# A one-core layer kernel: GpSimd's computing steps behind the routing go to VectorE and ScalarE, and one load moves

## The chip, the cores and the metric

The kernel runs on one core of a Trainium2 chip. The metric is the device time of one execution in microseconds (us). The core has TensorE (PE in the profile; PEld is its weight load), VectorE (DVE), ScalarE (ACT), GpSimd (POOL) and SyncE (SP), which here only issues DMAs. Each engine works through its own instructions in program order and waits for the others by semaphores.

## The reference

One transformer layer for 512 tokens of width 2048, float32. Three mixers run on one input projection, their outputs go through a projection, are added to the input and normed. A router then gives each token two of 32 experts, and the experts' weighted outputs are added and normed again:

```python
x = layer_norm(ALPHA * x + mix, ln1_g, ln1_b)
probs = softmax(x @ wg_r + bg_r)              # 4 groups, the best one is taken
e_val, e_idx = top_k(expert logits in that group, 2)
gates = g_val * softmax(e_val)
for each expert e, on the tokens routed to it:
    h = silu(xb @ w_gate[e]) * (xb @ w_up[e])
    ffn[token] += gate * (h @ w_down[e])
out = layer_norm(ALPHA * x + ffn, ln2_g, ln2_b)
```

## The kernel before, in words

The 512 tokens are four blocks (`b`) of 128 partitions; a block's row is 2048 wide, and `H` are its two halves, `Q` its four quarters. Matmuls are float32 in three parts: each operand is split by ScalarE into a rounded high part and by VectorE into the rest (lines 96 and 97 for weights, in the class `Ring`; 161 and 162 in `split`), and `mm3` (156 to 158) sums three products. Weights come in chunks of 512 KB. `Ring` holds a list of raw buffers and of split pairs: `pump` issues a chunk's load on the sync queue when a raw buffer is free (line 81) and splits it when a pair is free; `done` gives a used pair back and pumps. The order of all work is the order of the code, per engine.

**Routing** (lines 1099 to 1281). For each block `stats` (line 1106 on) makes the first norm's statistics (BATCH_NORM_STATS2, line 1006), `ln1` (1086) the normed rows, which go to the DRAM tensors `x1d` (one for each half); `route` makes one-hot choices in many small VectorE steps (lines 1129 to 1160), and `ranks`, `table` turn them into a table `idx` of the token for each expert and slot, with counts `cnt_i`. The last block's chain runs behind the last matmul of the projection. `xgs` are two buffers of 128 rows (in the slots M0 and B3) into which an expert's tokens are gathered; GpSimd clears both at line 1203. `exps` (1254 to 1257) has two exponentials of ScalarE behind two small GpSimd steps.

**Experts.** `gather(e)` (1322) issues two indirect DMAs on GpSimd's queue, for as many rows as the expert has tokens, rounded up to one of eight sizes; rows past that keep what the buffer held, and their gate is zero. From the third expert on GpSimd clears the buffer first (1330). `rows` transposes the rows on TensorE (1350) and applies the first norm's gain (1366, 1439). `up(e)` (1372) runs the gate and up matmuls for all 16 chunks; an expert with at most 64 tokens takes two matmuls for a piece of weights (1392, 1393), others three (`mm3`). `down(e)` (1414) runs the down projection, scales it by the gate table `gt` (1432), and `scatter` adds the rows to the DRAM tensors `yd` by indirect DMAs with an add (1340). `up(e)` is followed by `down(e - 1)`; at the end come `down(30)` and `down(31)`. The hooks of `up` put other steps between its chunks. `gates` is one of them, spread over chunks 0, 5 and 7 of the first expert's second half: a product over 128x256 (1284), a high part by ScalarE (1287), the rest of it by GpSimd (1288), eight matmuls (1292) that make the table of gates `gt`.

**Vectors.** `gb1` are two buffers (slots X7, B2) that hold the first norm's gain and bias from expert 12 on; VectorE applies them to the residual rows `z` during experts 13 to 28 (1562). At expert 29 the second norm's two vectors are loaded into the same slots (1557), on the sync queue, broadcast to all partitions, 1 MB each.

**The end** (from line 1577). The sums of the experts are read back from `yd` into `ys` (1581): seven reads on the sync queue, one on GpSimd's; a read of a half waits for the last scatter into that half. Then the second norm: `add` (1632) adds the sums to `z` and sums the row, `mean` (1589), `squares` (ScalarE, 1641), `root` (1594, 1595), `refine` (1600 to 1608) sharpens the root, `norm` (1613) and `scale_dve` (1620) apply it on VectorE in halves and store. A part goes to the other engines: block 3's adds to GpSimd (`add_pool`, 1635) with ScalarE's `total` (1638), block 1's norm and the last quarter of block 3 to ScalarE (`norm_act`, 1625) and GpSimd (`gain`, 1629).

Of the kernel before, what the change touches and what calls it, by code (L numbers as in the profile page):

```python
# [9 lines left out]
F32 = mybir.dt.float32  # L10
# [3 lines left out]
AF = mybir.ActivationFunctionType  # L14
OP = mybir.AluOpType
# [5 lines left out]
P = 128  # L21
T = 512
NB = T // P
DM = 2048
KD = DM // P
NE = 32
# [11 lines left out]
EPS2 = EPS / ALPHA ** 2  # L38
# [96 lines left out]
def _build(tc, nc, ctx, I, out):  # L135
# [8 lines left out]
    def slot(tag, shape, dt=F32):  # L144
        cnt[0] += 1
        return bp.tile([P] + list(shape), dt, tag=tag, name=f"{tag}_{cnt[0]}")
# [6 lines left out]
    act = nc.scalar.activation  # L153
# [73 lines left out]
    for k2 in range(8):  # L227
        t = slot(f"X{k2}", [2, 2, 512], F32R)
# [48 lines left out]
    def bcast(ap, n):  # L277
        return bass.AP(tensor=ap.tensor, offset=ap.offset, ap=[[0, P], [1, n]])
# [566 lines left out]
    def scale(b, Pn, s):  # L845
        nc.vector.reciprocal(s, s)
        ts(Pn[b], Pn[b], s, None, op0=OP.mult)
# [234 lines left out]
    def wide(ap, shape, axis):  # L1082
        return ap.unsqueeze(axis).to_broadcast([P] + list(shape))
# [115 lines left out]
    ring.add([r1[:, 0, :]], once=True)  # L1199
    ring.pump()  # L1200
    xgs = [slot(t, [DM]) for t in ("M0", "B3")]
    for t in xgs:
        nc.gpsimd.memset(t, 0.0)


    SIZES = (16, 24, 32, 40, 48, 64, 80, P)
# [46 lines left out]
    def exps():  # L1253
        nc.gpsimd.tensor_tensor(g4, lga[:, :, 0:4], wide(gm, [NB, 4], 2), op=OP.subtract)
        act(g4, g4, AF.Exp)
        nc.gpsimd.tensor_tensor(dlt, m2, m1, op=OP.subtract)
        act(e1, dlt, AF.Exp)

    weave(rt_, ranks())
    exps()  # L1260
    tt(oa[:, L], oh4[:, 0, L], oh4[:, 1, L], op=OP.add)
    mm(o3[:, 0:NE], afterr, oa[:, L], start=False, stop=True)
    mm(oc[:, 0:NE], onesr, oa[:, L], start=False, stop=True)
# [17 lines left out]
    gt = carve(NE)  # L1281

    def gates():
        nc.gpsimd.tensor_tensor(gv, oh, wide(gate, [2 * NB, NE], 2), op=OP.mult)
        hl = tp[:, 0:512].rearrange("p (i a e) -> p i a e", a=2, e=NE)
        yield
        act(hl[:, :, 0], gv, AF.Copy)
        nc.gpsimd.tensor_tensor(hl[:, :, 1], gv, hl[:, :, 0].bitcast(F32), op=OP.subtract)
        yield
        o = aux()  # L1290
        for i in range(2 * NB):
            mm(o[:, 0:2 * NE], ohr[:, i // NB, i % NB], hl[:, i].rearrange("p a e -> p (a e)"),
               start=i == 0, stop=i == 2 * NB - 1)
        nc.vector.tensor_copy(gt, o[:, 0:NE])
        tt(gt, gt, o[:, NE:2 * NE], op=OP.add)
        yield
# [25 lines left out]
    def gather(e):  # L1322
        def move(n):
            for i in range(2):
                nc.gpsimd.indirect_dma_start(out=xgs[e % 2][0:n, H[i]], out_offset=None, in_=x1d[i][:],  # L1325
                                             in_offset=off(idx[0:n, EX[e]:EX[e] + 1]),
                                             bounds_check=T - 1, oob_is_err=False)
        if e:
            if e > 1:
                nc.gpsimd.memset(xgs[e % 2], 0.0)  # L1330
            sized(e, move)
        else:

            move(32)
            with tc.If(nc.gpsimd.value_load(cnt_i[0:1, EX[0]:EX[0] + 1]) > 32):
                move(P)
# [183 lines left out]
    ring.pump(nc.scalar)  # L1520
    later = []
    ring.done()
    for e in range(NE):
        if e and e + 2 < NE:
            gather(e + 2)
# [25 lines left out]
        if e == NE - 3:  # L1551
            for entry in ers:
                entry[1] = True
        if e in (12, 29):
            gb1 = [slot("X7", [DM]), slot("B2", [DM])]
            for t, name in zip(gb1, ("ln1_g", "ln1_b") if e == 12 else ("ln2_g", "ln2_b")):
                nc.sync.dma_start(t, bcast(I[name], DM))
        if 13 <= e < 29:

            b, s = (e - 13) // 4, slice((e - 13) % 4 * 512, ((e - 13) % 4 + 1) * 512)  # L1560
# [8 lines left out]
        elif e < NE - 1:  # L1569
            down(e - 1)  # L1570
    down(NE - 2)
    down(NE - 1)

    lng2, lnb2 = gb1


    Q = [slice(i * 512, (i + 1) * 512) for i in range(4)]
    ys = [[slot(t, [DM]) for t in ts] for ts in (("M0", "B3"), ("B4", "X1"), ("B7", "X2"), ("X6", "X3"))]

    for i, b in ((0, 0), (0, 1), (0, 2), (1, 0), (1, 1), (0, 3), (1, 2), (1, 3)):  # L1580
        (nc.gpsimd if (i, b) == (0, 2) else nc.sync).dma_start(ys[b][1][:, H[i]], yd[i][b * P:(b + 1) * P])
    sums = carve(NB, 12)
    nc.scalar.preload_act_table_set("natural_log_exp_and_others")

    def col(b, i):
        return sums[:, b, i:i + 1]

    def mean(b):
        ts(col(b, 8), col(b, 0), col(b, 1), -1.0 / DM, op0=OP.add, op1=OP.mult)

    def root(b):

        r = rs[:, b:b + 1]
        act(r, col(b, 9), AF.Ln, scale=1.0 / DM, bias=eps2_c)
        act(r, r, AF.Exp, scale=-0.5)
# [16 lines left out]
        for s in parts:  # L1612
            stt(ys[b][1][:, s], z[b][:, s], col(b, 8), lng2[:, s], op0=OP.add, op1=OP.mult)

    def store(b, s):
        nc.sync.dma_start(out[b][:, s], z[b][:, s])

    def scale_dve(b, parts):
        for s in parts:
            stt(z[b][:, s], ys[b][1][:, s], rs[:, b:b + 1], lnb2[:, s], op0=OP.mult, op1=OP.add)  # L1620
            store(b, s)

    def norm_act(b, parts):
        for s in parts:
            act(z[b][:, s], z[b][:, s], AF.Identity, scale=rs[:, b:b + 1], bias=col(b, 7))

    def gain(b, s):
        for t, op in zip((lng2, lnb2), (OP.mult, OP.add)):
            nc.gpsimd.tensor_tensor(z[b][:, s], z[b][:, s], t[:, s], op=op)

    def add(b, s, i):
        stt(z[b][:, s], z[b][:, s], 1.0, ys[b][1][:, s], op0=OP.mult, op1=OP.add, accum_out=col(b, i))

    def add_pool(b, s):
        nc.gpsimd.tensor_tensor(z[b][:, s], z[b][:, s], ys[b][1][:, s], op=OP.add)

    def total(b, s, i):
        act(ys[b][0][:, s], z[b][:, s], AF.Copy, accum_out=col(b, i))

    def squares(b):  # L1640
        act(ys[b][0], z[b], AF.Square, bias=col(b, 8), accum_out=col(b, 9))

    def run(*seq):

        for f in seq:
            if callable(f):
                f()
            else:
                next(f, None)

    for b in range(3):
        add(b, H[0], 0)
    add(0, H[1], 1)
    mean(0)
    squares(0)
    root(0)
    norm(0, H[:1])
    add(1, H[1], 1)
    mean(1)
    squares(1)  # L1660
    root(1)
    add_pool(3, H[0])
    total(3, H[0], 0)
    add_pool(3, H[1])
    f = refine(0)
    run(f, lambda: norm(0, H[1:]), f, f, f)
    scale_dve(0, H[:1])
    for _ in refine(1):
        pass
    norm_act(1, H[:1])  # L1670
    gain(1, H[0])
    add(2, H[1], 1)
    mean(2)
    squares(2)
    root(2)
    total(3, H[1], 1)
    norm_act(1, H[1:])
    gain(1, H[1])
    scale_dve(0, H[1:])
    norm(2, H[:1])  # L1680
    f = refine(2)
    run(f, f, f, f)
    scale_dve(2, H[:1])
    mean(3)
    squares(3)
    root(3)
    store(1, H[0])
    norm(2, H[1:])
    scale_dve(2, H[1:])
    norm(3, H[:1])  # L1690
    f = refine(3)
    run(f, f, f, f, f)
    scale_dve(3, H[:1])
    store(1, H[1])
    norm_act(3, Q[3:])
    gain(3, Q[3])
    norm(3, Q[2:3])
    scale_dve(3, Q[2:3])
    store(3, Q[3])


# ---- launch: one core; the host only lays the inputs out
# [69 lines left out]
```

## Time and profile before

| what | us |
|---|---|
| median of 3 timed runs | 1944.67 |
| lowest and highest of them | 1938.79, 1944.82 |
| the profiled execution | 1938.76 |
| its span, first to last instruction | 1937.0 |
| TensorE busy | 1815.3 (94%) |
| VectorE busy | 1422.5 (73%) |
| ScalarE busy | 1260.0 (65%) |
| GpSimd busy | 317.4 (16%) |

The rows below come from the profiled execution. A row of the timeline has the start (us from the span's start), the duration, the engine, the line of the kernel, the operation, what it writes and reads by the program's names, shapes, the count, and in square brackets how long the engine was idle before it and who ended that wait. Tiles are named by their slots (X, B, M, whl, wraw) or by DRAM tensors. Busy times of different engines overlap, so they do not add up to the span.

### The profile page before, as it was taken

Reading aid. Unit: us, or ns where it says so; the run is one execution under the profiler, and the core shown is the slowest. Engines: PE = TensorE matmul, PEld = TensorE weight load, DVE = VectorE, ACT = ScalarE, POOL = GpSimd, SP = SyncE. Lnnn points to the kernel's source line nnn. Section 1 sums busy time; section 2 is a strip of 40 time slices with the busy share of each in tenths; the row PEclk is TensorE's granted clock in tenths of the full one; section 3 lists DMA queues with packets and bytes.
Section 4 is the critical chain, followed back from the end, with each engine's and each line's share of the span. In section 5 each row is a group of like instructions: output and inputs, shape, how many; then the busy total and the mean of one; then the engine's idle time right before and its main releaser. Section 6 shows DMA issues by size and latency. Waiting matters only on the chain.

```text
span 1937.0 us, 25438 instructions
## 1 busy us (share of the span) xinstructions
PE 1815.3 (94%) x8235; PEld 1367.7 (71%) x8236; DVE 1422.5 (73%) x2031; ACT 1260.0 (65%) x1763; POOL 317.4 (16%) x235
## 2 busy tenths in 40 slices
PE   9999999999999996899999999999999999999990
PEld 7888888887887895666666666666766666667650
DVE  5656433566564457888988889898898989988857
ACT  4533363635452224788878888787887878888853
POOL 1000000020000002313122221321222222121014
PEclk9999999999999997899999999999999999999995
DMA  7222222223154225799999999999999999999984
GB/s 252 97 87 77 77 77 91 95 87 131 44 191 175 87 88 192 260 351 381 389 394 382 390 345 388 395 379 392 385 365 395 391 390 383 377 389 386 327 297 171
DMA packets 142426, 510.75 MB, mean 264 GB/s; under 512 B 18608, under 2 KB 18656, under 8 KB 141216
## 3 DMA queue, kind: packets, MB, share of 16 engines
q1 hardware_dynamic: 130752, 476.64, 65.7%
q0 software_dynamic: 10912, 30.26, 5.9%
q8 instruction: 93, 1.52, 0.3%
q10 hardware_dynamic: 576, 1.57, 0.2%
q14 instruction: 93, 0.76, 0.1%
HBM read 488.53 MB, written 22.02 MB: 264 GB/s over the span
## 4 chain that ended last, share of the span: by engine, by line
issue 49%; PE 36%; POOL 8%; DVE 3%; DMA 3%; POOLq 1%; ACT 0%; ACTq 0%; DVEq 0%
PE acc L156 10%; PE acc L157 10%; PE acc L158 10%; POOL yd L1340 2%; POOL B L1325 2%; DMA x1d<-B 1%; POOL M L1325 1%; DMA yd<-M,idx 1%; POOL M L1330 1%; POOL B L1330 1%; PE aux L495 1%; PE acc L860 1%; POOLq L1310 1%; DVE B L1620 0%; POOLq L1316 0%
## 5 line engine op out<-in xcount | busy, mean ns | idle before, releaser
L97 DVE TENSOR_TENSOR whl<-X,whl 128x1024 fp32r<-128x1024 f32 x312 | 376.6, 1218 | 98.9 <-ACT whl L96 97.2
L97 DVE TENSOR_TENSOR whl<-wraw,whl 128x1024 fp32r<-128x1024 f32 (+1 forms) x222 | 269.3, 1215 | 226.3 <-ACT whl L96 219.6
L96 ACT ACTIVATE whl<-wraw 128x1024 fp32r<-128x1024 f32 (+1 forms) x222 | 235.2, 1062 | 219.2 <-PE acc L157 93.6
L96 ACT ACTIVATE whl<-X 128x1024 fp32r<-128x1024 f32 x312 | 331.1, 1075 | 59.5 <-PE acc L158 40.3
L1393 PE MATMUL acc<-whl,B 128*128 128x512 f32 x696 | 287.2, 413 | 15.3 <-DVE whl L97 15.3
L1392 PE MATMUL acc<-whl,B 128*128 128x512 f32 x696 | 293.8, 422 | 0.9 <-DVE B L162 0.8
L1340 POOL DMA_INDIRECT yd<-M,idx x64 | 90.5, 1414 | 826.3 <-ACT M L1432 826.3
L1393 PEld LDWEIGHTS acc<-whl,B 128*128 128x128 f32 x696 | 131.4, 189 | 86.3 <-DVE whl L97 58.9
L158 PE MATMUL acc<-whl,B 128*128 128x512 f32 (+1 forms) x480 | 181.2, 377 | 0.0
L157 PE MATMUL acc<-whl,B 128*128 128x512 f32 (+1 forms) x424 | 165.8, 391 | 14.7 <-DVE whl L97 14.6
L156 PE MATMUL acc<-whl,B 128*128 128x512 f32 (+1 forms) x424 | 179.2, 423 | 0.1
L1392 PEld LDWEIGHTS acc<-whl,B 128*128 128x128 f32 x696 | 131.6, 189 | 30.3 <-issue 4.1
L156 PE MATMUL acc<-X,whl 128*128 128x512 f32 x384 | 151.0, 393 | 0.0
L157 PE MATMUL acc<-X,whl 128*128 128x512 f32 x384 | 149.7, 390 | 0.3 <-DVE X L162 0.3
L158 PE MATMUL acc<-X,whl 128*128 128x512 f32 x384 | 149.6, 390 | 0.0
L1428 PE MATMUL acc<-X,X 128*128 128x512 f32 x308 | 141.1, 592 | 0.0
L97 DVE TENSOR_TENSOR X<-X,X 128x1024 fp32r<-128x1024 f32 x105 | 127.8, 1217 | 17.6 <-ACT X L96 13.3
L96 ACT ACTIVATE X<-X 128x1024 fp32r<-128x1024 f32 x105 | 112.6, 1072 | 20.4 <-PE acc L158 15.0
L1432 ACT ACTIVATE M<-acc,X 128x512 f32<-128x512 f32 x128 | 87.3, 682 | 50.8 <-PE acc L1428 44.1
L157 PEld LDWEIGHTS acc<-whl,B 128*128 128x128 f32 x424 | 80.5, 190 | 47.8 <-DVE whl L97 26.9
L1393 PE MATMUL acc<-X,B 128*128 128x512 f32 x232 | 97.9, 422 | 11.0 <-DVE X L97 11.0
L158 PEld LDWEIGHTS acc<-whl,B 128*128 128x128 f32 x480 | 91.0, 190 | 15.7
(461 smaller groups left out, 3696.4 us busy)
## 6 DMA issues: line engine op xcount, KB each, us to landing
X<-w_down SPq DMA_DIRECT2D x169, 512.0 KB, 10.2
X<-w_gate SPq DMA_DIRECT2D x160, 512.0 KB, 9.9
X<-w_up SPq DMA_DIRECT2D x160, 512.0 KB, 9.0
wraw<-w_gate SPq DMA_DIRECT2D x69, 512.0 KB, 9.9
wraw<-w_up SPq DMA_DIRECT2D x69, 512.0 KB, 9.1
wraw<-w_in SPq DMA_DIRECT2D x64, 512.0 KB, 3.3
wraw<-w_down SPq DMA_DIRECT2D x64, 512.0 KB, 10.1
B<-w_up SPq DMA_DIRECT2D x27, 512.0 KB, 8.9
```

The source lines that it names most:

```text
L96: nc.scalar.activation(h[:, s], r[:, s], AF.Copy)
L97: nc.vector.tensor_tensor(l[:, s], r[:, s], h[:, s].bitcast(F32), op=OP.subtract)
L156: mm(o, a[0], b[0], start=start, stop=False)
L157: mm(o, a[0], b[1], start=False, stop=False)
L158: mm(o, a[1], b[0], start=False, stop=stop)
L1325: nc.gpsimd.indirect_dma_start(out=xgs[e % 2][0:n, H[i]], out_offset=None, in_=x1d[i][:], in_offset=off(idx[0:n, EX[e]:EX[e] + 1]), bounds ...
L1330: nc.gpsimd.memset(xgs[e % 2], 0.0)
L1340: nc.gpsimd.indirect_dma_start(out=yd[i][:], out_offset=off(index), in_=y[:, H[i]], in_offset=None, bounds_check=T - 1, oob_is_err=False, ...
L1392: mm(o, x, wk[0], start=k == 0, stop=False)
L1393: mm(o, x, wk[1], start=False, stop=k == KD - 1)
L1428: mm(o, hfs[e % 2][:, k * P:(k + 1) * P], w[:, cs], start=k == 0, stop=k == 3)
L1432: act(yts[-1][:, n * 512:(n + 1) * 512], o, AF.Copy, scale=gt[:, EX[e]:EX[e] + 1])
```

## The change

The clears of `xgs` leave GpSimd: the two buffers are cleared once, by ScalarE, behind `exps`, as a copy of a broadcast constant scaled by zero; `gather` clears nothing any more. The two GpSimd operations of `gates` are VectorE's. The second norm's vectors are loaded by `vectors` between `down(30)` and `down(31)` in the order of the code rather than at expert 29. All eight reads of the sums are on the sync queue, first halves first. The second norm is VectorE's alone but for ScalarE's squares and roots: all adds, norms and scales, in a plainer order, with the last block's scales in quarters.

```diff
@@ -1199,8 +1199,6 @@
     xgs = [slot(t, [DM]) for t in ("M0", "B3")]
-    for t in xgs:
-        nc.gpsimd.memset(t, 0.0)
@@ -1258,6 +1256,8 @@
     exps()
+    for t in xgs:
+        act(t, one_c.to_broadcast([P, DM]), AF.Copy, scale=0.0)
@@ -1281,11 +1281,11 @@
-        nc.gpsimd.tensor_tensor(gv, oh, wide(gate, [2 * NB, NE], 2), op=OP.mult)
+        tt(gv, oh, wide(gate, [2 * NB, NE], 2), op=OP.mult)
         hl = tp[:, 0:512].rearrange("p (i a e) -> p i a e", a=2, e=NE)
         yield
         act(hl[:, :, 0], gv, AF.Copy)
-        nc.gpsimd.tensor_tensor(hl[:, :, 1], gv, hl[:, :, 0].bitcast(F32), op=OP.subtract)
+        tt(hl[:, :, 1], gv, hl[:, :, 0].bitcast(F32), op=OP.subtract)
@@ -1326,8 +1326,6 @@
         if e:
-            if e > 1:
-                nc.gpsimd.memset(xgs[e % 2], 0.0)
             sized(e, move)
@@ -1520,6 +1518,14 @@
+    def vectors(*names):
+
+        ts = [slot("X7", [DM]), slot("B2", [DM])]
+        for t, name in zip(ts, names):
+            nc.sync.dma_start(t, bcast(I[name], DM))
+        return ts
+
@@ -1551,10 +1557,8 @@
-        if e in (12, 29):
-            gb1 = [slot("X7", [DM]), slot("B2", [DM])]
-            for t, name in zip(gb1, ("ln1_g", "ln1_b") if e == 12 else ("ln2_g", "ln2_b")):
-                nc.sync.dma_start(t, bcast(I[name], DM))
+        if e == 12:
+            gb1 = vectors("ln1_g", "ln1_b")
@@ -1569,16 +1573,15 @@
     down(NE - 2)
+    lng2, lnb2 = vectors("ln2_g", "ln2_b")
     down(NE - 1)
-
-    lng2, lnb2 = gb1
-    for i, b in ((0, 0), (0, 1), (0, 2), (1, 0), (1, 1), (0, 3), (1, 2), (1, 3)):
-        (nc.gpsimd if (i, b) == (0, 2) else nc.sync).dma_start(ys[b][1][:, H[i]], yd[i][b * P:(b + 1) * P])
+    for i in range(2):
+        for b in range(NB):
+            nc.sync.dma_start(ys[b][1][:, H[i]], yd[i][b * P:(b + 1) * P])
@@ -1612,91 +1615,46 @@
...
+    def scale(b, parts=H):
         for s in parts:
             stt(z[b][:, s], ys[b][1][:, s], rs[:, b:b + 1], lnb2[:, s], op0=OP.mult, op1=OP.add)
+            nc.sync.dma_start(out[b][:, s], z[b][:, s])
+
+    def add(b, i):
+        s = H[i]
         stt(z[b][:, s], z[b][:, s], 1.0, ys[b][1][:, s], op0=OP.mult, op1=OP.add, accum_out=col(b, i))
...
+    def stats(b):
+        add(b, 1)
+        ts(col(b, 8), col(b, 0), col(b, 1), -1.0 / DM, op0=OP.add, op1=OP.mult)
         act(ys[b][0], z[b], AF.Square, bias=col(b, 8), accum_out=col(b, 9))
...
+        act(r, col(b, 9), AF.Ln, scale=1.0 / DM, bias=eps2_c)
+        act(r, r, AF.Exp, scale=-0.5)
+
+    def refine(b):
+
+        r, v, t = rs[:, b:b + 1], col(b, 10), col(b, 11)
+        ts(v, col(b, 9), 1.0 / DM, EPS2, op0=OP.mult, op1=OP.add)
+        stt(t, r, v, r, op0=OP.mult, op1=OP.mult)
+        ts(t, t, -0.5, 1.5, op0=OP.mult, op1=OP.add)
+        tt(r, r, t, op=OP.mult)
+
+    for b in range(NB):
+        add(b, 0)
+    stats(0)
     norm(0, H[:1])
...
+    stats(1)
+    norm(0, H[1:])
+    stats(2)
+    refine(0)
+    scale(0)
+    stats(3)
+    for b in range(1, NB):
+        norm(b)
+        refine(b)
+        scale(b, Q if b == NB - 1 else H)
```

`add_pool`, `total`, `norm_act`, `gain`, `scale_dve`, `store`, `mean`, `root` and the old `refine` are gone with the order that called them.

## Rows read from the trace of the kernel before

**Rows 1.** Busy us by stretch (length, engines with counts, clock, DMA share, GB/s): experts.

```profile
1322.41:1428.83 106.42, 103.52 (x442) 74.28 (x441) 93.40 (x113) 87.36 (x121) 21.73 (x15) 1.00 1.02 381
1735.31:1841.76 106.45, 103.55 (x442) 74.24 (x441) 90.96 (x109) 87.47 (x121) 16.42 (x12) 1.00 0.98 358
```

**Rows 2.** Timeline of VectorE and GpSimd, the routing's last block.

```profile
747.10 2.96 DVE L1006 BATCH_NORM_STATS2 X<-B 128x6 f32<-128x256 f32 x1
748.21 1.82 POOL L1203 MEMSET B<- 128x2048 f32 x1
```

**Rows 3.** Groups by line (busy us, mean ns, idle before), VectorE, 730 to 746 us.

```profile
L1006 DVE BATCH_NORM_STATS2 X<-B 128x6 f32<-128x256 f32 x2 | 0.8, 420 | 0.0
```

**Rows 4.** Timeline of ScalarE, GpSimd and TensorE, end of the routing.

```profile
752.36 2.09 ACT L1086 ACTIVATE B<-B,X 128x2048 f32<-128x2048 f32 x1 [1.15 <-DVE X L1123]
756.76 0.21 ACT L1257 ACTIVATE X<-X 128x4 f32<-128x4 f32 x1 [2.20 <-POOL X L1256]
760.71 1.92 POOL L1325 DMA_INDIRECT M<-x1d,idx  x1 [3.98 <-DVE X L1511]
766.99 1.30 PE L1350 MATMUL aux<-identr,M 128*128 128x128 f32 x5 [7.38 <-DMA M<-x1d,idx]
```

**Rows 5.** Timeline of GpSimd, VectorE and TensorE, around the gate table.

```profile
795.52 5.61 POOL L1288 TENSOR_TENSOR X<-X,X 128x256 fp32r<-128x256 f32 x1 [5.31 <-ACT X L1287]
753.76 0.35 DVE L1243 TENSOR_TENSOR X<-X,aux 128x192 f32<-128x192 f32 x1 [0.31 <-PE aux L1233]
797.60 1.21 DVE L97 TENSOR_TENSOR X<-M,X 128x1024 fp32r<-128x1024 f32 x1
801.19 1.06 PE L1292 MATMUL aux<-X 128*128 128x64 f32 x4 [5.37 <-POOL X L1288]
```

**Rows 6.** Busy us by stretch, behind the gate table's wait.

```profile
802.00:808.00 6.00, 6.00 (x22) 4.94 (x22) 1.80 (x4) 2.64 (x4) 0.00 (x0) 0.57 0.23 76
```

**Rows 7.** Timeline of VectorE and GpSimd, one expert's clear (one of 30).

```profile
1085.71 1.23 DVE L97 TENSOR_TENSOR whl<-wraw,whl 128x1024 fp32r<-128x1024 f32 x1 [2.35 <-ACT whl L96]
1085.57 2.30 POOL L1330 MEMSET B<- 128x2048 f32 x1
```

**Rows 8.** Timeline of the sync queue, the last weights (two halves of a chunk).

```profile
1873.34 0.86 SPq L81 DMA_DIRECT2D wraw<-w_down  x2
```

**Rows 9.** Line 1557, the four loads of the norms' vectors.

```profile
DMA to landing us min/median/max: 8.0/10.1/11.5
```

**Rows 10.** Line 1581, the eight reads of the experts' sums.

```profile
DMA to landing us min/median/max: 3.3/5.2/8.0
```

**Rows 11.** Timeline of VectorE and GpSimd, the end.

```profile
1897.37 1.23 DVE L1632 SCALAR_TENSOR_TENSOR B<-B,B 128x1024 f32<-128x1024 f32 x1 [1.04 <-DMA B<-yd]
1900.09 1.22 DVE L1632 SCALAR_TENSOR_TENSOR B<-B,X 128x1024 f32<-128x1024 f32 x1
1900.51 6.29 POOL L1635 TENSOR_TENSOR B<-B,X 128x1024 f32<-128x1024 f32 x2 [8.87 <-DMA X<-yd]
1901.55 3.06 DVE L1613 SCALAR_TENSOR_TENSOR B<-B,X,X 128x1024 f32<-128x1024 f32 x1
1927.10 0.15 DVE L1600 TENSOR_SCALAR X<-X 128x1 f32<-128x1 f32 x1
1927.99 0.16 DVE L1608 TENSOR_TENSOR X<-X 128x1 f32<-128x1 f32 x1
1931.05 1.63 DVE L1620 SCALAR_TENSOR_TENSOR B<-X,X,B 128x512 f32<-128x512 f32 x1
```

**Rows 12.** Groups by line, VectorE, 1896 to 1937 us.

```profile
L1613 DVE SCALAR_TENSOR_TENSOR X<-B,X,X 128x1024 f32<-128x1024 f32 (+1 forms) x4 | 7.7, 1919 | 0.0
L1620 DVE SCALAR_TENSOR_TENSOR B<-X,X,B 128x1024 f32<-128x1024 f32 (+1 forms) x4 | 7.6, 1910 | 0.1
L1602 DVE SCALAR_TENSOR_TENSOR X<-X 128x1 f32<-128x1 f32 x4 | 4.8, 1194 | 0.3
L1620 DVE SCALAR_TENSOR_TENSOR B<-B,X,B 128x1024 f32<-128x1024 f32 x2 | 2.6, 1280 | 0.0
```

More of the change, by code (lines that the diff above doesn't have):

```diff
@@ L1613, in norm @@
             stt(ys[b][1][:, s], z[b][:, s], col(b, 8), lng2[:, s], op0=OP.add, op1=OP.mult)
-    def store(b, s):
-        nc.sync.dma_start(out[b][:, s], z[b][:, s])
-    def scale_dve(b, parts):
+    def scale(b, parts=H):
         for s in parts:
             stt(z[b][:, s], ys[b][1][:, s], rs[:, b:b + 1], lnb2[:, s], op0=OP.mult, op1=OP.add)
[L1621 to L1631, printed above, removed]
-        stt(z[b][:, s], z[b][:, s], 1.0, ys[b][1][:, s], op0=OP.mult, op1=OP.add, accum_out=col(b, i))
[L1634 to L1640, printed above, removed]
-        act(ys[b][0], z[b], AF.Square, bias=col(b, 8), accum_out=col(b, 9))
@@ L1643, in run @@
[L1643 to L1656, printed above, removed]
-    norm(0, H[:1])
[L1658 to L1699, printed above, removed]
+            nc.sync.dma_start(out[b][:, s], z[b][:, s])
+    def add(b, i):
+        s = H[i]
+        stt(z[b][:, s], z[b][:, s], 1.0, ys[b][1][:, s], op0=OP.mult, op1=OP.add, accum_out=col(b, i))
+    def stats(b):
+        add(b, 1)
+        ts(col(b, 8), col(b, 0), col(b, 1), -1.0 / DM, op0=OP.add, op1=OP.mult)
+        act(ys[b][0], z[b], AF.Square, bias=col(b, 8), accum_out=col(b, 9))
+        r = rs[:, b:b + 1]
+        act(r, col(b, 9), AF.Ln, scale=1.0 / DM, bias=eps2_c)
+        act(r, r, AF.Exp, scale=-0.5)
```

## The prediction, made before the changed kernel ran

> **What bounds the kernel now.** I read the busy time by stretch first, then the timeline of three places where GpSimd (POOL in the rows) computes: the routing, the first expert, the end. The long expert stage is bound by TensorE together with the splits that feed it: over three experts each, TensorE is busy 103.5 of 106.4 us and VectorE 91 to 93 [rows 1]. These two stretches are cut at the same instruction of experts 16 to 18 and 28 to 30; each holds one expert with the longer matmul form. The second has the load of the second norm's two vectors (1 MB each) in its middle, the first has none, and they differ by 0.03 us. Outside that stage the work is a chain with one engine at a time, so a microsecond taken from the engine that is last there moves the end by a microsecond.
>
> **The change, part by part.** The sum is made against the profiled execution: span 1937.0, with what lies around it 1938.76.
>
> *Two clears leave GpSimd in the routing.* While GpSimd clears the two row buffers, VectorE's BATCH_NORM_STATS2 of the last token block takes 2.96 us and ends at 750.06, just as the second clear does (748.21 + 1.82) [rows 2]. Its two siblings some microseconds earlier mean 0.42 [rows 3]. The chain from this statistic to the ranks, to the first gather and to the first transposes is VectorE's, so all that is late in it is on the path: 2.96 - 0.42 = 2.5 us come back. The lowest value is nothing (if the stall has another cause), the highest 2.9, the whole excess with the tensor_scalar queued ahead. I take 2.5.
>
> The Trainium skill (SBUF — State Buffer, Who interferes with whom) says that a VectorE instruction with at most one SBUF input, outside the two-port modes, does not contend with GpSimd, and that one with two inputs contends only with a GpSimd instruction that reads. By that a clear, which only writes, would not hold a statistic with one input, and the sum would lose these 2.5 us; the row speaks for a stall all the same, so I keep it and give the rule a rival below.
>
> *The clears go to ScalarE*, behind the two exponentials. A ScalarE pass over 128x2048 takes 2.09 us, and ScalarE comes free of the exponentials at 756.97; the first gather starts at 760.71 and its rows reach TensorE at 766.99 [rows 4]. Shifted by the 2.5 us gained, the clears would run from 754.5 to 758.7, the first buffer being ready at 756.6 and its gather due at 758.2. So the gather covers them by 1.6 us; the three splits behind them on ScalarE start at 758.7 rather than 754.4 and need three times 1.04, so end before 762, ahead of the first rows at 764.5. Cost nothing; with the cover gone it would be at most 2 x 2.09 = 4.2.
>
> *The gate table goes to VectorE.* GpSimd's subtraction takes 5.61 us from 795.52, and TensorE stands idle for 5.37 us until 801.19 for it [rows 5]. On VectorE it is queued ahead of the split that starts at 797.60. For its 128x256 the nearest row is a 128x192 tensor_tensor of 0.35 us; I take 0.35 (0.3 to 0.5). It ends at 797.95 instead of 801.13, and TensorE resumes 3.2 us sooner. The product ahead of it also goes to VectorE, which is full there: 0.35 us against the gain. Net -2.9. Behind that wait TensorE runs at the lower of its two clocks: the granted clock is 0.57 on average over 802 to 808, 1.2 GHz for most of it, and TensorE is busy for all 6.0 us [rows 6]. The new wait is 797.95 - 795.82 = 2.1 us. If the clock stays at 2.4 GHz through it, up to 6.0 / 2 = 3 us more come back. No row tells whether a wait of 2.1 us brings the fall; I count no gain from it and keep it as a rival. Lower bound of the step: nothing, should TensorE then wait for VectorE's splits.
>
> *Thirty clears leave the expert stage.* A split that runs beside such a clear takes 1.23 us, and the clear 2.30 [rows 7]. Next to the 1.21 of [rows 5], where no clear runs, VectorE loses nothing. The gathers start some 2.3 us sooner and have an expert's time of slack. Worth 0 (0 to 0.6, thirty times 0.02).
>
> *The vectors' load* moves from expert 29, where it cost 0.03 us [rows 1], to behind the last weights, which the sync queue issues from 1873.34 to 1874.20 [rows 8]. The queue is past its weights then; behind the vectors stand only the reads of the sums, which wait for the scatters anyway. The earlier loads of vectors took 8.0 to 11.5 us [rows 9], so they land by 1886 or 1887, ten microseconds ahead of their first use. Cost 0. Its two megabytes do share the DMA engines with the scatter of expert 30 and the last weights; the bound for that is with the next rival.
>
> *The end.* All reads of the sums are now on the sync queue, first halves first; one such read takes 3.3 to 8.0 us [rows 10]. I leave the arrival that starts the last chain at 1897.37, with -1 to +3.5 for the range (the new order has fewer reads in front of that half, but more beside the last scatter). From there VectorE works through without GpSimd. The rows give: add, mean and one half of a norm 2.72 (1897.37 to 1900.09); four refining operations 0.89 (1927.10 to 1927.99); the half-row operations are 1.28 when GpSimd is idle (mean 1280 of the two scales) and 2 to 3 us beside it, as the 3.06 at 1901.55 inside GpSimd's 6.29 us from 1900.51 [rows 11, 12]. Behind the arrival stand 4 x 2.72 = 10.9; four more norm halves, 4 x 1.28 = 5.1; six scale halves 7.7; four quarters at half of that, 2.6; refining 4 x 0.89 = 3.6: 29.8 us, to 1927.2. Before, the last operation ends at 1932.68 (1931.05 + 1.63). ScalarE's squares and roots are due 10 us before their use. The stores behind are alike. So -5.5 (-2.0 if the reads are late by 3.5, -6.5 if early).
>
> Sum: -2.5 - 2.9 - 5.5 = -10.9, so 1927.9 against the profiled execution. The three timed runs lie at 1938.79 and 1944.67 to 1944.82; the profiled one is with the lower. From the median the same sum gives 1933.8. No row says which group the median of after falls into, so I predict the middle, 1931, with 1928 to 1934 as the forecast's own range.
>
> **The rivals.**
>
> 1. *The clock stays up* in the gate table's shorter wait: 3 us more, -13.9: 1925 to 1931. For it speaks that the wait is 2.1 instead of 5.4 us; against it that the trace has no wait of that length, in a stretch as busy, through which it held.
>
> 2. *What is freed is given back by data.* The reads of the sums are late by 3.5 us because the vectors, four first reads and the scatters are on the DMA engines together, and the gate table comes when TensorE would wait for VectorE's splits anyway. Then -2.5 - 0 - 2.0 = -4.5: 1934 to 1940. For it: reads at 8.0 us exist [rows 10]; VectorE has no idle time around the gate table. Against it: the last scatter has fewer weights beside it than any other.
>
> 3. *The routing's stall is not the clears'.* Some other thing holds the statistic for 2.5 us and stays. Then -8.4: 1930 to 1936. Against it: its end is the second clear's to 0.03 us. That is what the skill's rule on one-input operations would make of it (the page named above).
>
> 4. *Slower: the long VectorE rows of the end are not GpSimd's doing*, but come with ScalarE's squares and the stores. VectorE now holds all the work, and at the long means it is too much. Eight norm halves at 1.919, six scales at 1.910, four quarters at 0.96, four adds with means at 2.72 - 1.28 = 1.44, and each refining a microsecond longer (one of its operations has a mean of 1194 ns, where all four take 0.89 above) [rows 12]: 15.4 + 11.5 + 3.8 + 5.8 + 7.6 = 44.1, to 1941.5, which is 8.8 later than before. With the same doubt on the other two places nothing comes back there: 1948 to 1953. It decides from a mean of 1.6 us per half row: the end's gain of 5.5 us is spread over 16 half rows, 0.34 each. Against it: each long row lies inside a GpSimd tensor_tensor, and the rows of 1.28 lie outside.
>
> 5. *It doesn't do what it says*: GpSimd's waits and its descriptor work for the gathers and scatters remain, and it is they that the chain follows: 1937 to 1946.
>
> **How the numbers follow.** Forecast 0.55; the clock stays up 0.15; given back 0.14; the stall stays 0.06; slower 0.05; no effect 0.05. A difference under 0.3% (5.8 us) can't be told from none. Faster: 0.55 + 0.15 + 0.06 and 0.04 of the second rival make 0.80; same: 0.10 of it and most of the fifth, 0.14; slower 0.06. The range goes from 1924 (clock up, lower group) to 1941 (given back, upper group).
>
> **What would show it.** BATCH_NORM_STATS2 of the last block at 0.42 us and the first transposes 2.5 us sooner; TensorE's wait for the gate table at about 2 us; equal experts; no VectorE half row above 1.4 us behind the last scatter, and 29 to 31 us from the arrival of the first second-half read to the last scale. Wrong it would be if that arrival came after 1900, if the first gather waited for ScalarE, or if half rows stayed near 1.9 us with GpSimd idle.

## The result and the profile after

The changed kernel takes 1928.39 us in the median of nine runs (1927.74 to 1933.83), the kernel before 1943.28 beside it (1937.58 to 1947.2). The ratio is 0.9937, with an interval of 0.9927 to 0.9948. The runs of before lie in two groups, and its median here fell into the upper one: of its 56 runs beside the later experiments, the 11 above 1944 us show a mean granted clock of TensorE of 0.975 or 0.976, the others, up to 1943 us, 0.978 to 0.981. The medians of these later runs are 1939.1 to 1939.6, and against that after is 11 us faster. The forecast was 1931.0, with a range of 1924 to 1941.

The two profiled executions took 1938.76 us before and 1928.39 after, with spans of 1937.0 and 1926.6. The rest of this section compares these two. The first rows are the timeline of after around the routing's last block, ScalarE's clears and the first transposes (start, duration, engine, line, operation, what it writes and reads; in brackets the idle time ahead of it and who ended it). They answer to [rows 2] and [rows 4].

```profile
747.10 0.42 DVE L1006 BATCH_NORM_STATS2 X<-B 128x6 f32<-128x256 f32 x1
...
754.21 1.89 ACT L1260 ACTIVATE M<-one_c 128x2048 f32<-128x2048 f32 x1
756.00 1.89 ACT L1260 ACTIVATE B<-one_c 128x2048 f32<-128x2048 f32 x1
757.80 1.04 ACT L96 ACTIVATE whl<-wraw 128x1024 fp32r<-128x1024 f32 x1
758.04 1.01 POOL L1325 DMA_INDIRECT M<-x1d,idx  x1 [3.98 <-DVE X L1509]
758.88 1.23 DVE L97 TENSOR_TENSOR whl<-wraw,whl 128x1024 fp32r<-128x1024 f32 x1 [0.93 <-ACT whl L96]
762.67 1.08 PE L1348 MATMUL aux<-identr,M 128*128 128x128 f32 x4 [5.73 <-DVE whl L97]
766.91 2.06 PE L1348 MATMUL aux<-identr,M 128*128 128x128 f32 x8 [3.15 <-DVEq L1503]
767.07 0.73 DVE L1364 TENSOR_SCALAR M<-aux,X 128x128 f32<-128x128 f32 x2 [4.69 <-DVEq L1503]
769.42 0.77 PE L1390 MATMUL acc<-whl,B 128*128 128x512 f32 x1 [0.46 <-DVE B L162]
```

The last of these rows is TensorE's first matmul with an expert's weights; before, it was this one:

```profile
772.92 0.78 PE L1392 MATMUL acc<-whl,B 128*128 128x512 f32 x1
```

The statistic that took 2.96 us takes 0.42, and the first gather starts at 758.04 instead of 760.71. TensorE's transposes come in fours, 4.3, 1.0 and 4.3 us sooner than before, and its first matmul with weights 3.5 us sooner. The clears are 0.1 us behind the exponential and done before the gather, as planned, but ScalarE's splits come behind them and VectorE waits 0.93 us for the first.

Next the gate table, in the timeline of after and by stretch of its clock (length, busy time and count of each engine, granted clock, DMA share, GB/s); [rows 5, 6] are the same place of before.

```profile
795.41 0.42 DVE L1288 TENSOR_TENSOR X<-X,X 128x256 fp32r<-128x256 f32 x1
795.88 1.08 PE L1292 MATMUL aux<-X 128*128 128x64 f32 x8 [2.24 <-DVE X L1288]
```

```profile
797.63:801.05 3.42, 3.42 (x11) 2.64 (x10) 2.66 (x5) 2.44 (x4) 1.91 (x1) 0.50 0.81 289
801.05:807.00 5.95, 5.95 (x35) 5.17 (x34) 5.05 (x8) 3.75 (x6) 1.52 (x1) 1.00 0.97 329
```

TensorE waits 2.24 us instead of 5.37. Its clock still falls to 1.2 GHz, 0.5 in the first of these rows, but is back at 2.4 GHz after 3.41 us; before, it was low for 10.24, of which 6.0 us came behind the end of the wait (801.19 to 807.21).

The experts are as they were: the same two stretches as in [rows 1], shifted by the 6 us won until then, are 106.40 us both, against 106.42 and 106.45.

```profile
1316.00:1422.40 106.40, 103.49 (x442) 74.24 (x441) 93.77 (x112) 87.23 (x121) 19.70 (x12) 1.00 1.01 379
1729.20:1835.60 106.40, 103.48 (x442) 74.20 (x441) 91.12 (x109) 87.60 (x121) 15.99 (x10) 1.00 0.93 340
```

Then the hand-over to the end: ScalarE's last row of the down projection (the last evacuation, below), the last two scatters on GpSimd and the reads of the sums on the sync queue; after first, then before, with its last scatter and the read on GpSimd's queue.

```profile
1883.13 0.69 ACT L1430 ACTIVATE M<-acc,X 128x512 f32<-128x512 f32 x1 [2.75 <-PE acc L1426]
...
1879.68 1.32 POOL L1338 DMA_INDIRECT yd<-M,idx  x1 [5.49 <-DMA yd<-M,idx]
1884.10 1.31 POOL L1338 DMA_INDIRECT yd<-M,idx  x1 [3.10 <-ACT M L1430]
...
1882.85 0.33 SPq L1584 DMA_DIRECT2D B<-yd  x1
1883.22 1.56 SPq L1584 DMA_DIRECT2D X<-yd  x3
1890.39 0.32 SPq L1584 DMA_DIRECT2D B<-yd  x1
```

```profile
1888.70 0.69 ACT L1432 ACTIVATE M<-acc,X 128x512 f32<-128x512 f32 x1 [2.75 <-PE acc L1428]
...
1889.66 1.31 POOL L1340 DMA_INDIRECT yd<-M,idx  x1 [4.85 <-ACT M L1432]
1890.55 1.10 POOL L1581 DMA_DIRECT2D X<-yd  x1
...
1892.84 0.32 SPq L1581 DMA_DIRECT2D B<-yd  x1
```

The first read of a second half is issued when the last scatter has landed. That is 3.2 us behind the scatter's start before (1889.66 to 1892.84) and 6.3 after (1884.10 to 1890.39), where four reads of first halves run beside the scatter; before, two were issued ahead of it and a third, on GpSimd's queue, 0.9 us behind its start. The read itself is quicker after: the add that waits for it starts 3.4 us behind its issue (1890.39 to 1893.75), 4.5 before (1892.84 to 1897.37). Together the arrival is 1.95 us later, counted from the last evacuation.

Last the end itself, VectorE's timeline of after, against [rows 11, 12].

```profile
1893.75 1.22 DVE L1625 SCALAR_TENSOR_TENSOR B<-B,B 128x1024 f32<-128x1024 f32 x1 [1.24 <-DMA B<-yd]
1896.47 1.22 DVE L1625 SCALAR_TENSOR_TENSOR B<-B,X 128x1024 f32<-128x1024 f32 x1
...
1901.34 2.48 DVE L1620 SCALAR_TENSOR_TENSOR B<-B,X,B 128x1024 f32<-128x1024 f32 x2
1903.74 1.22 DVE L1625 SCALAR_TENSOR_TENSOR B<-B,X 128x1024 f32<-128x1024 f32 x1
...
1919.77 2.74 DVE L1620 SCALAR_TENSOR_TENSOR B<-X,X,B 128x512 f32<-128x512 f32 x4
```

No half row is above 1.28 us. From the first add of a second half to VectorE's end it is 1893.75 to 1922.51, 28.76 us; before, 1897.37 to 1932.68, 35.31.

The span is 10.4 us shorter, and these parts, from the two traces, make it up: routing -2.2 (TensorE's last matmul ahead of the gate table's wait ends that much sooner), the wait -3.1, the clock behind it -1.2 (the same matmuls behind the wait take 9.0 us instead of 10.2), the experts +0.9, the late reads +1.95, the end -6.55, what follows VectorE's last operation -0.2.

### The profile page after: what moved, and what is told of

Read it like the earlier page. It is cut to its first block, busy times and chain, and to the rows that moved or that the text cites. A ratio compares the mean times of both kernels' runs of the same rounds, so it can differ in the third digit from the quotient of the medians.

```text
span 1926.6 us, 25404 instructions
## 1 busy us (share of the span) xinstructions
PE 1815.6 (94%) x8235; PEld 1366.7 (71%) x8236; DVE 1415.2 (73%) x2041; ACT 1258.6 (65%) x1758; POOL 242.0 (13%) x192
## 4 chain that ended last, share of the span: by engine, by line
issue 48%; POOL 5%; DMA 2%; DVE 2%; POOLq 1%; ACT 0%; PE 0%; DVEq 0%; ACTq 0%
POOL yd L1338 2%; DMA yd<-M,idx 2%; POOL M L1325 2%; POOL B L1325 2%; POOLq L1310 1%; DVE B L1620 0%; DVE X L1616 0%; POOLq L1316 0%; DVE whl L97 0%; DMA X<-w_up 0%; DVE B L1625 0%; DMA B<-yd 0%; ACT whl L96 0%; DVE B L162 0%; POOLq L1338 0%
```

## The experiments

Each is the kernel after with one edit, unless another is named. A plus or minus is against the median of after, 1928.39, which did not run again beside them; the kernel before did. "Last evacuation" is ScalarE's last row of the down projection, behind which only the scatter and the end remain: 1888.70 before, 1883.13 after.

**The gate table back to GpSimd.**

```diff
-        tt(gv, oh, wide(gate, [2 * NB, NE], 2), op=OP.mult)
+        nc.gpsimd.tensor_tensor(gv, oh, wide(gate, [2 * NB, NE], 2), op=OP.mult)
-        tt(hl[:, :, 1], gv, hl[:, :, 0].bitcast(F32), op=OP.subtract)
+        nc.gpsimd.tensor_tensor(hl[:, :, 1], gv, hl[:, :, 0].bitcast(F32), op=OP.subtract)
```

> The changed kernel with the gate table's two operations back on GpSimd, all else as changed. If TensorE's wait for the gate table was on the path: the wait grows from 2.24 to about 5.4 us, the stretch at the lower clock from 3.4 to about 10 us, and the time rises by 4 to 5 us (3.1 of waiting, 1.2 or more of clock) against the changed kernel's 1928.4, so 1932 to 1934; and the runs spread over several us again, if the clock's stretch behind a longer wait is what spread the runs of the kernel before. If the expert stage gives the wait back (VectorE's splits get ahead meanwhile): under 1 us, 1928 to 1929.

Measured: 1931.86 (1931.62 to 1932.46), 3.5 above after, a little less than the 4 to 5 expected. The spread that was expected to come back did not: 0.8 us over five runs.

```profile
793.78 5.19 POOL L1288 TENSOR_TENSOR X<-X,X 128x256 fp32r<-128x256 f32 x1 [8.86 <-ACT X L1287]
799.03 1.91 PE L1292 MATMUL aux<-X 128*128 128x64 f32 x8 [5.36 <-POOL X L1288]
```

The wait of 5.36 us is back, with 10.24 us at the lower clock (from 795.50), and the last evacuation is at 1886.41, 3.3 later. What is lost at this wait thus stays lost to the end of the expert stage: the experts have no slack that gives it back.

**The same alone, on the kernel before** (only the two lines above, the other way).

> The kernel before with nothing but the gate table's two operations moved to VectorE. If the gate wait and the clock's fall behind it are on the path: 4 to 5 us faster than the kernel before in like executions, and if that fall is what spread its runs over 1938 to 1947, these runs lie within 2 us of each other. If the spread has another source, it stays.

Measured: 1934.87 over 12 runs, before 1939.58 beside it, -4.7; ratio 0.9984, 0.997 to 0.9997. In its profiled execution the wait is 2.24 us and the lower clock lasts 3.41 us, as in after. By the medians the step is worth 3.5 to 4.7 us, and its two parts, 3.1 of wait and 1.2 of clock, make 4.3; by the ratio of this run it is 3.1, with 0.6 to 5.8 as the interval. The runs still lie 9 us apart (1932.9 to 1942.2), so their spread has another source than this fall of the clock.

**The routing's clears once on GpSimd, as before, none on ScalarE.**

```diff
     xgs = [slot(t, [DM]) for t in ("M0", "B3")]
+    for t in xgs:
+        nc.gpsimd.memset(t, 0.0)
...
-    for t in xgs:
-        act(t, one_c.to_broadcast([P, DM]), AF.Copy, scale=0.0)
```

> The changed kernel with the two clears once on GpSimd, at their old place, and none on ScalarE. If GpSimd's clear is what stalled VectorE: the last block's BATCH_NORM_STATS2 is 2.9 to 3.0 us instead of 0.42 and the first expert starts about 2 us later, 1930 to 1931 by the median. If the stall had another cause: 0.42 us stays and the time does not rise, 1927.5 to 1929.

Measured: 1931.32 (1929.84 to 1932.3), +2.9. The timeline of VectorE, then GpSimd:

```profile
747.05 3.10 DVE L1135 TENSOR_SCALAR X<-dsc,X 128x8 f32<-128x8 f32 x1
747.19 2.97 DVE L1006 BATCH_NORM_STATS2 X<-B 128x6 f32<-128x256 f32 x1
...
748.30 1.82 POOL L1203 MEMSET B<- 128x2048 f32 x1
```

The statistic is at 2.97 us again and ends with the second clear (750.16 and 750.12). So the stall is the clears', and rival 3 falls. The first operation in the stall is the tensor_scalar ahead of the statistic, 3.10 us instead of the 0.23 it takes in after; the statistic stands behind it in VectorE's queue, and whether the clear held it too or only the tensor_scalar, no row shows. The Trainium skill (SBUF — State Buffer, Who interferes with whom) says that a VectorE instruction with at most one SBUF input does not contend with GpSimd outside the two-port modes. These rows do not decide on it, since no row shows in which mode the tensor_scalar ran.

**The clears ahead of ScalarE's exponentials** instead of behind them.

```diff
+    for t in xgs:
+        act(t, one_c.to_broadcast([P, DM]), AF.Copy, scale=0.0)
     exps()
-    for t in xgs:
-        act(t, one_c.to_broadcast([P, DM]), AF.Copy, scale=0.0)
```

> The changed kernel with ScalarE's two clears ahead of the two exponentials, where ScalarE waits 2.2 us for GpSimd. In the changed kernel VectorE waits 0.93 us for ScalarE's first split behind the clears. If that wait is on the path: VectorE's splits start 0.9 us sooner and the whole is 0.5 to 0.9 us faster, 1927.5 to 1928. If the gather or the branch behind it sets the start: no change.

Measured: 1925.91 over four runs (1924.98, 1925.68, 1926.13, 1929.63), 2.5 below after, where 0.5 to 0.9 was expected; the intervals of the two ratios overlap (0.9905 to 0.9942, and 0.9927 to 0.9948 for after). The clears fill ScalarE's wait of 2.2 us for the exponentials' inputs:

```profile
752.40 1.89 ACT L1259 ACTIVATE M<-one_c 128x2048 f32<-128x2048 f32 x1
754.20 1.89 ACT L1259 ACTIVATE B<-one_c 128x2048 f32<-128x2048 f32 x1
...
756.20 1.04 ACT L96 ACTIVATE whl<-wraw 128x1024 fp32r<-128x1024 f32 x1
```

The three splits start at 756.20 instead of 757.80, though the last statistic was 0.7 us later in this execution. The first matmul of the experts comes 0.6 us sooner, counted from that statistic (769.53 - 747.82 against 769.42 - 747.10). The rows thus show 0.6 of the 2.5, in the slowest of the four runs (1929.63 is the profiled one); the rest is within what the runs differ by.

**The expert clears put back** on GpSimd, 30 of them.

```diff
         if e:
+            if e > 1:
+                nc.gpsimd.memset(xgs[e % 2], 0.0)
             sized(e, move)
```

> The changed kernel with GpSimd's clear back in each gather from the third expert on (30 clears of 2.3 us). If they are hidden: the experts' period stays 34.06 us, VectorE's splits stay at 1.21 to 1.23 us beside them, and the time is the changed kernel's within 0.6 us. If they hold VectorE as the clears in the routing did: up to 2 us an expert, 60 us in all.

Measured: 1928.53 (1927.87 to 1930.04), the time of after. A split beside a clear takes 1.23 us as in [rows 7], and its neighbours 1.22: this two-input operation is not held by a clear. From the first expert's down projection to the last evacuation it is 1054.71 us here, 1054.63 in after, 1053.72 in before, and 1053.22 to 1056.27 in nine other kernels without these clears (the upper two, a3_vectors_29 and b3_clears_first, with 3.41 us at the lower clock in the last expert, which the execution with the clears has too). The 0.9 us that the experts seem to lose in after lie inside what single executions differ by.

**The vectors back at expert 29**, with the end of after.

```diff
         if e == 12:
             gb1 = vectors("ln1_g", "ln1_b")
+        if e == 29:
+            lng2, lnb2 = vectors("ln2_g", "ln2_b")
...
-    lng2, lnb2 = vectors("ln2_g", "ln2_b")
     down(NE - 1)
```

> The changed kernel with the second norm's vectors loaded at expert 29, as before. In the changed kernel the scatter of expert 31's first half waited for the DMA of expert 30's scatter (until 1879.7 rather than 1877.7), the first reads came close to the last scatter, and that scatter took 6.3 us instead of 3.2. If the vectors beside them did that: both scatters take about 3.2 us again, the first second-half read lands about 2 us sooner, 1926 to 1927. If the four first reads alone did it: only the first scatter is sooner and the time stays, 1928 to 1929. If the load costs the expert stage its bytes' time: later by up to 5 us.

Measured: 1928.22 (1927.47 to 1933.62), the same. Without the vectors beside it, the scatter ahead of the last is released by ScalarE again, but the last scatter is as slow as in after:

```profile
1880.15 1.31 POOL L1338 DMA_INDIRECT yd<-M,idx  x1 [4.71 <-ACT M L1430]
1886.31 1.31 POOL L1338 DMA_INDIRECT yd<-M,idx  x1 [4.85 <-ACT M L1430]
...
1892.31 0.32 SPq L1585 DMA_DIRECT2D B<-yd  x1
```

6.0 us, with the four first reads beside it and no vectors. The delay is not the vectors'; that it is the reads' is what the two experiments on their order, below, show.

**The old end**, lines from `Q` on as in before, all else as in after.

> The changed kernel with the old end (GpSimd adds and gains, ScalarE sums and norms, one read on GpSimd's queue, the old order), all else as changed. If GpSimd beside VectorE was the end's cost: VectorE half rows of 2 to 3.4 us are back, and from the first second-half read to the last VectorE operation it takes 35 us instead of 28.8; since the reads come about 2 us sooner, the time rises by 4.5 to 6.5 us, 1933 to 1935. If all of the end's gain is from the reads' order: no more than 2 us.

Measured: 1934.86 over 11 runs (1932.34 to 1940.06), +6.5. From the first add of a second half it takes 35.5 us (1890.71 to 1926.24), and the long rows are back where GpSimd computes:

```profile
1894.73 2.35 POOL L1638 TENSOR_TENSOR B<-B,X 128x1024 f32<-128x1024 f32 x1 [9.26 <-DMA X<-yd]
...
1894.88 3.28 DVE L1616 SCALAR_TENSOR_TENSOR B<-B,X,X 128x1024 f32<-128x1024 f32 x1
1898.09 2.29 DVE L1605 SCALAR_TENSOR_TENSOR X<-X 128x1 f32<-128x1 f32 x1
...
1916.96 1.27 DVE L1616 SCALAR_TENSOR_TENSOR X<-B,X,X 128x1024 f32<-128x1024 f32 x1
```

Even an operation on one column is held for 2.29 us. Of the 6.8 us by which the end is longer, the old order of the reads gives 2.4 back: the arrival comes 8.2 us behind the last evacuation instead of 10.6. The profiled execution, the lowest of the 11 runs, is 4.0 us above that of after; the rest of the 6.5 lies in the spread of these runs.

**The new end alone, on the kernel before** (vectors' load, reads and second norm of after; clears and gate table stay GpSimd's).

> The kernel before with only the end of after: the vectors loaded behind the last weights, the eight reads on the sync queue, the second norm on VectorE alone. The clears and the gate table stay GpSimd's. Theory: the end is worth what undoing it cost (a4_old_end, +6.5 us), so -4.5 to -6.5 us against before: 1932.5 to 1935, and the runs lie within 3 us of each other instead of 8 to 9, since the spread went with the old end in the runs so far. Rival (the freed time of the end is given back once the routing and the gates come late by 5 us again, since the data of the sums comes with the last scatter's reads, not with TensorE): less than -3 us. Rival on the spread (it belongs to the routing or the gates and only looked tied to the end): the runs still lie 6 us or more apart.

Measured: 1934.85 over 11 runs, before 1939.56, -4.7; ratio 0.9973, 0.9962 to 0.9985. The first add of a second half:

```profile
1901.02 1.23 DVE L1627 SCALAR_TENSOR_TENSOR B<-B,B 128x1024 f32<-128x1024 f32 x1 [0.68 <-DMA B<-yd]
```

The end takes 28.75 us from there, and that add comes 10.4 us behind the last evacuation, as in after (10.6) and not as in before (8.7). So the end wins 6.5 us and hands 1.8 back to its own reads: -4.7. Ten of the eleven runs lie within the 3 us that were expected, one is 5 us above them.

**Eight idle GpSimd operations beside the new end**, whose output nobody reads.

```diff
+    idle = slot("B0", [DM])
+    for _ in range(8):
+        nc.gpsimd.tensor_tensor(idle[:, H[0]], lng2[:, H[0]], lnb2[:, H[0]], op=OP.mult)
     for b in range(NB):
         add(b, 0)
```

> The kernel after, with eight GpSimd tensor_tensor operations of 128x1024 ahead of the second norm, which only read the vectors of the second norm and write a buffer that nobody reads. GpSimd takes some 3.1 us for one, so they run from about 1887 to 1912, beside the first half of the end. Theory: VectorE's half rows beside them go from 1.25 to between 1.8 and 3 us, 10 to 14 of them, so that the end grows by 6 to 10 us: 1934 to 1938, and the rows behind the last of them are 1.25 again. Rival 4 of the prediction (the long rows came with ScalarE's squares and the stores, not with GpSimd): half rows stay at 1.25 and the time at 1928.

Measured: 1941.41 over ten runs (1939.83 to 1946.26), +13, more than the 6 to 10 that were expected. With these operations beside it nothing is left of the gain: the ratio to before is 1.0004 (0.999 to 1.0018). GpSimd's row, then VectorE's:

```profile
1883.75 25.76 POOL L1646 TENSOR_TENSOR B<-X,B 128x1024 f32<-128x1024 f32 x8
...
1897.39 3.35 DVE L1625 SCALAR_TENSOR_TENSOR B<-B,B 128x1024 f32<-128x1024 f32 x1
...
1907.47 3.12 DVE L1616 SCALAR_TENSOR_TENSOR B<-B,X,X 128x1024 f32<-128x1024 f32 x1
1910.52 1.21 DVE L1625 SCALAR_TENSOR_TENSOR B<-B,X 128x1024 f32<-128x1024 f32 x1
```

All eight half rows up to GpSimd's end at 1909.51 take 3.0 to 3.35 us, the next 1.21. ScalarE's squares of 2.00 us each run on both sides of that point, the stores (from 1914.11) beside short rows alone. Rival 4 falls: the squares and the stores do not make the rows long, GpSimd's operations do. The Trainium skill (SBUF — State Buffer, Who interferes with whom) says that a VectorE instruction with two SBUF inputs contends with a GpSimd instruction that reads SBUF. This trace agrees: 3.0 to 3.35 us beside such instructions, 1.21 without.

**Two first reads, then second halves**, only the order on the sync queue changed.

```diff
-    for i in range(2):
-        for b in range(NB):
+    for i, b in ((0, 0), (0, 1), (1, 0), (1, 1), (0, 2), (0, 3), (1, 2), (1, 3)):
```

> The changed kernel with two instead of four reads of first halves ahead of the last scatter's end (the order of the reads as before, all on the sync queue). If the four first reads slow the last scatter: it takes 3.2 to 4.5 us instead of 6.3 and the first second-half read lands 1 to 2 us sooner, but blocks 2 and 3 wait for their first halves, so the time is between 1 us faster and 1 us slower. If the vectors do it: the scatter stays at about 6 us.

Measured: 1931.43 (1930.27 to 1932.39), +3.0, where no more than 1 us either way was expected. The last scatter is quicker, with the vectors still loaded beside it: 3.9 us from its start to the next read. But VectorE's adds of blocks 2 and 3 stand ahead of the second halves in its queue and now wait for their reads:

```profile
1881.88 1.31 POOL L1338 DMA_INDIRECT yd<-M,idx  x1 [3.08 <-ACT M L1430]
1885.79 0.32 SPq L1583 DMA_DIRECT2D B<-yd  x1
...
1893.25 1.23 DVE L1624 SCALAR_TENSOR_TENSOR B<-B,X 128x1024 f32<-128x1024 f32 x1 [6.64 <-DMA X<-yd]
```

So the last scatter lands sooner beside two reads than beside four, and to win by it the order of the adds has to follow.

**Reads and adds both in the order of use.**

```diff
+    for i, b in ((0, 0), (0, 1), (1, 0), (1, 1), (0, 2), (1, 2), (0, 3), (1, 3)):
...
-    for b in range(NB):
+    for b in range(2):
         add(b, 0)
...
+    add(2, 0)
     stats(2)
...
+    add(3, 0)
     stats(3)
```

> The kernel after with the reads of the sums in the order of use, two blocks at a time (first halves of blocks 0 and 1, their second halves, then the same of 2 and 3), and the first-half adds of blocks 2 and 3 moved behind the first norms of blocks 0 and 1, so that VectorE does not wait for them. Theory (the four first reads beside the last scatter slow it: 6.3 us to the second-half reads in after, 3.9 in b2_two_first_reads with two): the first add of a second half comes 2 us sooner, and the time is 1926 to 1927; b2 lost 3 us only because adds of blocks 2 and 3 stood ahead on VectorE. Rival (the late reads do not decide, VectorE or the stores do): 1928, or above 1929 if VectorE waits for the reads of blocks 2 and 3 in the middle of the norm.

Measured: 1927.95 (1926.36 to 1933.69), 0.4 below after, so the expected gain of 1 to 2 us is not there. The arrival does move: the first add of a second half comes 7.5 us behind the last evacuation instead of 10.6.

```profile
1892.13 1.23 DVE L1624 SCALAR_TENSOR_TENSOR B<-B,B 128x1024 f32<-128x1024 f32 x1 [2.41 <-DMA B<-yd]
...
1897.44 1.22 DVE L1624 SCALAR_TENSOR_TENSOR B<-B,X 128x1024 f32<-128x1024 f32 x1
```

From there it takes 31.04 us instead of 28.76 (1892.13 to 1923.17). The 2.3 us are the two adds of 1.14 that stood in front of the arrival, in time that VectorE had to wait anyway, and now stand behind it. Of the 3.1 us won, 0.9 remain in this pair of executions, which is less than runs differ by.

**Both: this order, and the clears ahead of the exponentials.**

> c4_reads_order, and the two clears ahead of ScalarE's exponentials as in b3_clears_first. Theory: the two gains lie in different stages and add: b3 measured -2.5 against after, c4 is expected at -1 to -2, so 1924 to 1925. Rival (the gain of one is given back in the expert stage or by the scatters): no better than the better of the two, 1926.

Measured: 1927.06 over six runs (1924.99 to 1927.84), ratio to before 0.9929 (0.9913 to 0.9945). The two edits do not add to the 1924 to 1925 that were expected, and the interval overlaps that of after. Its lowest run and b3's are the lowest of all kernels, 1924.99 and 1924.98, and both medians are below that of after, by 1.3 and 2.5 us; whether either is really better than after is open.

## Why the prediction was right, step by step

**The routing's clears**: predicted -2.5, measured -2.2 in the profile and 2.9 when undone. The clears were the cause, as predicted. The prediction put the stall on the statistic, with the tensor_scalar ahead as the upper bound; it is that tensor_scalar that stands first in it (3.10 us in a2_clears_gpsimd, 0.23 in after), so whether a clear holds the statistic itself is open. The sign that was named, the first transposes 2.5 us sooner, came out as 4.3, 1.0 and 4.3 for three groups of four; the first matmul with weights is 3.5 us sooner, the end of the stretch ahead of the gate table 2.2. The cover for ScalarE's clears was counted against the gather alone, where it held. The splits behind them were counted against the first rows; VectorE waited 0.93 us for one all the same, and moving the clears wins 0.6 in the rows. That cost is at most a microsecond, far from the bound of 4.2.

**The gate table**: predicted -2.9 with the clock not counted; measured 3.1 of wait and 1.2 of clock, 3.5 to 4.7 when done or undone alone. The wait was right (2.1 predicted, 2.24 measured), the tensor_tensor of 128x256 takes 0.42 us and not 0.35. The mis-sized term is the clock. It was put as all or nothing, 3 us or none; what came is in between, 3.4 us at the lower clock behind the wait instead of 6.0. That the clock stays up, rival 1, is seen in one execution alone, that of b2_two_first_reads.

**Expert clears and vectors' load**: predicted 0 each, measured none beyond what the runs differ by (1928.53 with the clears back, 1928.22 with the vectors back).

**The arrival of the last chain**: predicted unchanged with up to +3.5 for more reads beside the last scatter, measured +1.95: 3.1 for the last scatter, less 1.2 by which the read behind it is quicker. Rival 2 named the vectors, the first reads and the scatters together; the experiments leave the first reads alone as the cause (6.0 us with four of them and no vectors in a3_vectors_29, 3.9 and 3.2 with two of them and the vectors in b2_two_first_reads and c4_reads_order). Its other half, a gate table that gives nothing back, did not happen.

**The end**: predicted 29.8 us from the arrival, measured 28.76, so -6.55 instead of -5.5. Part of the sum added durations, but VectorE's half rows of 1.28 us start 1.20 apart: behind the two scales from 1901.34 the next add starts at 1903.74. Over the ten norm and scale halves that were counted at 1.28 that is 0.8 us; three of the four groups of add, mean and half a norm take 2.6 instead of 2.72, 0.4 together, and the four quarters take 0.2 more than was counted. Rivals 4 and 5, long rows without GpSimd and no effect, fall with these rows.

Against the profiled execution the sum was -10.9 and the outcome -10.4. That the two are so near is in part luck: the clock and the end came out 2.3 us larger than counted, the late reads and the experts of this pair of executions took 2.9 back. The forecast of 1931 lay 2.6 us high because it was put midway between the sums from the profiled execution, 1927.9, and from the median of before, 1933.8.

## What to carry to other kernels

Read what the engine that is last does while GpSimd computes. Here eight GpSimd operations of 25.8 us beside VectorE cost 13, two clears of 3.6 us cost 2.5 to 2.9, and even VectorE's operations on one column were held; 30 clears beside VectorE's splits cost nothing. So look at the rows beside them before moving anything. An operation that moved from a slow engine to a full one paid because another engine stood still for it, and the gain stayed because the stage behind has no slack. Work that fills a wait is free only there: moved behind the arrival that it waited for, it is paid in full.

## What the runs showed of the hardware that was not expected

The last scatter, an indirect DMA that adds, takes 3.2 to 4.0 us to land where two plain reads were issued ahead of its landing on the sync queue (before, b4_gates_alone and a4_old_end, each with a third on GpSimd's queue behind the scatter's start; b2_two_first_reads, c3_best, c4_reads_order) and 5.8 to 7.4 where four were (after and the seven other kernels with its order of reads).

In c2_gpsimd_beside, where VectorE and GpSimd both work on two inputs in SBUF, GpSimd's operations, of 3.2 us each, start 3.28 us apart, and so do VectorE's half rows beside them, one for one; alone such a row takes 1.2. Beside GpSimd's clears in the experts (before), VectorE's tensor_scalar of 128x128, which reads TensorE's output, takes 0.40 us in all 60 cases, as without a clear; beside those in the routing the tensor_scalar of 128x8 takes 3.10.

The lower clock behind the gate table's wait lasts 10.24 us behind a wait of 5.37 or 5.36 (before, a1_gates_gpsimd) but 6.83 behind one of 5.35 (c1_new_end_alone); behind 2.24 it lasts 3.41 in most executions, 6.83 in those of a2_clears_gpsimd, a3_vectors_29 and c4_reads_order, and in that of b2_two_first_reads the clock did not fall, which brought its matmuls behind the wait 1.6 us sooner than in after, counted from the wait's end. What decides among these was not found.

In after, VectorE starts its first gain 4.69 us behind its last split, and the trace puts that on its own queue at the branch of line 1503, which is not taken. With the clears moved (b3_clears_first) VectorE waits for TensorE there, and 7.08 us of TensorE are put on the same branch. What holds the two there is open.
